# The value projections of two linear-attention branches as two stages of seven block products

## The chip, the cores and the metric

The kernel runs on one core of a Trainium2 chip. A core has a matrix engine (TensorE, PE in the profile; its weight loads, PEld, run beside the matmuls), VectorE (DVE), ScalarE (ACT), GpSimd (POOL) and SyncE (SP); here SP issues the loads and POOL most stores. Operands lie in SBUF, 128 partitions wide; matmuls accumulate in PSUM banks of 128 x 512 float32. The metric is the device time of one execution in microseconds, lower is better.

## The reference

One layer of a decoder trunk, 1024 rows (SEQ) by 1024 channels (D), in float32. The input is normalised and modulated, and one projection feeds two branches that run on the same normalised rows:

```python
h = rms_norm(x, norm_w[l]) * (1.0 + scale[:, None, :]) + shift[:, None, :]
proj = h @ w_in[l]
hq, hf, hi, hz, gq, gk, gv, gz, ga, mg = jnp.split(proj, IN_OFFSETS, axis=-1)
y_h = hgrn2_branch(hq, hf, hi, hz, lb_all[l], hgrn_norm_w[l])
y_g = gla_branch(gq, gk, gv, gz, ga, gla_alpha_w[l], gla_alpha_b[l], gla_norm_w[l])
u_h = y_h @ w_branch[l, 0]
u_g = y_g @ w_branch[l, 1]
mg = jax.nn.sigmoid(mg.reshape(B, T, N_BRANCH, D_MODEL))
merged = mg[:, :, 0] * u_h + mg[:, :, 1] * u_g
x = x + gate[:, None, :] * (merged @ w_out[l])
```

Both branches are causal linear attentions with a decay per key channel (8 heads of 128 channels in HGRN, 4 heads of 128 key and 256 value channels in GLA), `S_t = diag(a_t) S_{t-1} + k_t v_t^T`, `o_t = S_t^T q_t`. The change touches `v` alone: `gv` (GLA) and `hi` (HGRN), each the product of the 1024 x 1024 matrix h and a 1024 x 1024 part of `w_in`. In GLA the decay alpha comes from a rank-16 projection (`ga`) through a log-sigmoid.

## The kernel before

**Arithmetic.** Every float32 operand of a large product is split into a high and a low part in a shorter matmul format (`split`, L195: L200 casts on ACT, L201 subtracts on DVE), and a product is three matmuls: high x high, high x low, low x high. h, transposed, is kept whole in this form (`h_hi[k]`, `h_lo[k]`, eight tiles of 128 channels x 1024 rows each) and also, as float32, in DRAM (`h_d`).

**Memory.** SBUF is handed out as 46 slots of 4 KB per partition (`Slots`); a slot that comes free goes to a later tile, and a tile whose store is still under way is freed with `sent=True`, so that its slot is taken up again later than others. `Halves` (`Q`) gives out half slots. PSUM: two tiles of two banks (`dtile`, 128 x 1024, names pd), one more such tile for attention scores (`sc_ps`), and two of one bank (`mtile`, names pm).

**Stages.** First come normalisation, modulation and transposes. Then `first_group` (L488; its matmuls are L372) computes six feature groups of 128 channels side by side, the four heads of q and the first two of k of GLA, in six banks: `acc0` (both pd tiles) and `sc_ps`; `qk_out` (L351) copies each finished half to the tiles `qk_t`. Behind it runs a stream of jobs, `Stream.go`. A job has a `load` (raw weights by DMA), a `prep` (the hi/lo split) and a `run` (its matmuls, which yields after each unit); `ahead` does the loads and preps of coming jobs, as far as slots are free. After each unit `weave` advances two other tracks: `side` (decay chain `alpha_side`, then the attention of one head after another; a yielded number is the count of units to wait, run at PACE 1.1) and `back` (preparation of the last stages: factors, weight sums, gates).

The jobs, in order: `First` (the q/k group); for each GLA head its k projection (heads 2 and 3), two gate projections z, and its values; for each HGRN head q, f, z, with the values of four heads at once ahead of heads 0 and 4. A projection `Feat` (L581) is 8 x 2 x 3 = 48 matmuls of 128 x 512. A value job computes rows x channels, so that h is the stationary operand:
- `Vblk` (GLA, one head, 256 channels): 8 row blocks x 8 k-blocks x 3 matmuls of 256 columns (L640, L641, L642); four row blocks share a pd tile, which ACT copies to SBUF (L645). Its end starts the head's attention.
- `Vblk2` (HGRN, four heads, 512 channels): 8 x 8 x 3 matmuls of 512 columns (L683 to L685), two row blocks to a pd tile, copied by L688.

The first value matmul starts at 137.2 us and the last of the GLA branch at 365.6; those of the HGRN branch lie between 390.0 and 665.7.

Last come the gates, the branch projections and the output projection (L1387, L1564). These three 1024 x 1024 x 1024 products are computed as seven half-size products each instead of eight (`PRODUCTS`): four of the seven take sums of weight blocks (`w_sums`, made on DVE and stored to DRAM by the back track), four take differences of activation blocks (`f_x` for h, by `factors`), and results are combined from the accumulators and snapshots of them.

**Order.** The opening up to `first_group` follows an order written out by hand. Behind it the program order of jobs, `ahead` and `weave` is handed to a scheduler, which settles each engine's order. Each engine works through its own instructions in order; semaphores hold an instruction until what it needs is there.

## Time and profile before

| | |
|---|---|
| median of 3 runs | 1208.71 us (1207.79 to 1209.38) |
| the profiled execution | 1209.15 us, its span 1207.4 us |
| mean granted TensorE clock | 0.996 |

| stretch, us | length | PE busy | DVE busy | ACT busy | clock | GB/s |
|---|---|---|---|---|---|---|
| 0 to 109.5: opening, q/k group | 109.5 | 100.3 | 57.3 | 64.8 | 0.97 | 218 |
| 109.5 to 389.8: GLA stream | 280.3 | 278.5 | 167.8 | 121.4 | 1.00 | 119 |
| 389.8 to 802.4: HGRN stream | 412.6 | 412.0 | 273.4 | 157.3 | 1.00 | 121 |
| 802.4 to 1207.4: last stages | 405.0 | 395.3 | 288.4 | 204.9 | 1.00 | 188 |

An execution is profiled once; its span runs from the first to the last instruction that the profile shows, and the time of the execution contains a little more. Busy time counts an engine's instructions, overlaps once. In the timeline a row reads: start, duration, engine, line, operation, output <- inputs, shape, how many such rows in a run (x), and in brackets the idle time ahead of it and what ended that. Matmuls are pipelined: the duration of one is longer than the distance to the next.

### The profile page before, as it was taken

To read this page: it belongs to the slowest core of one execution; us is meant where nothing else is said; L and a number is where in the kernel's file an instruction comes from. 1 tells how busy PE (TensorE), PEld (TensorE's weight loads), DVE (VectorE), ACT (ScalarE), POOL (GpSimd) and SP (SyncE) were. 2 spreads that over 40 slices of the span, in tenths; PEclk is the share of its full clock that TensorE was granted. 3 is DMA by queue.
4 is the path that set the end of the run, shared out by engine and by line. 5 is a ranking of instruction groups with operands and counts; after the bars stand their busy time and mean duration, and the time that the engine had idled before them with its cause. 6 is when DMAs were issued, how large, how long until landed. Compare 5 with 4: busy or idle time off the path is not lost.

```text
span 1207.4 us, 20861 instructions
## 1 busy us (share of the span) xinstructions
PE 1186.1 (98%) x8617; PEld 990.0 (82%) x8617; DVE 786.9 (65%) x1210; ACT 548.3 (45%) x798; POOL 94.6 (8%) x204
## 2 busy tenths in 40 slices
PE   7999999999999999999999999999999999999997
PEld 6777889889798888888888888877878888878886
DVE  4737444774857556777965455795654865988994
ACT  5646732434434244234333324455743544444554
POOL 4100000101101012011100000000120000000000
PEclk8999999999999999999999999999999999999999
DMA  9814000844544167355441212154797846435423
GB/s 324 276 70 140 19 19 19 280 153 147 172 141 147 62 211 241 117 167 165 134 175 43 65 52 71 36 175 157 251 340 263 269 153 213 132 106 175 167 100 134
DMA packets 130960, 183.51 MB, mean 152 GB/s; under 512 B 7467, under 2 KB 97633, under 8 KB 130866
## 3 DMA queue, kind: packets, MB, share of 16 engines
q1 hardware_dynamic: 117250, 136.87, 36.3%
q0 software_dynamic: 13568, 45.31, 9.7%
q8 instruction: 67, 1.10, 0.4%
q14 instruction: 27, 0.22, 0.1%
q10 hardware_dynamic: 48, 0.01, 0.0%
HBM read 132.87 MB, written 49.28 MB: 151 GB/s over the span
## 4 chain that ended last, share of the span: by engine, by line
issue 58%; PE 30%; POOL 5%; DVE 2%; DMA 2%; ACT 1%; SPq 0%; POOLq 0%; DVEq 0%; ACTq 0%
PE pd L1387 9%; PE sc_ps L1387 5%; PE pm L1387 5%; PE pd L1564 3%; POOL ws L1244 2%; PE sc_ps L1564 2%; PE pm L1564 1%; PE pd L581 1%; DMA b<-in_w_in_dram 1%; POOL yh L956 1%; PE pd L372 1%; DMA b<-in_x_dram 1%; POOL yg L956 0%; DMA yg<-b 0%; POOL fx L1210 0%
## 5 line engine op out<-in xcount | busy, mean ns | idle before, releaser
L581 PE MATMUL pd<-b,b 128*128 128x512 f32 x1632 | 387.4, 394 | 0.0
L581 PEld LDWEIGHTS pd<-b,b 128*128 128x128 f32 x1632 | 302.4, 188 | 64.9 <-issue 1.4
L1387 PE MATMUL pd<-b,b 128*128 128x512 f32 x720 | 173.6, 392 | 2.7 <-DVE b L993 1.0
L1387 PEld LDWEIGHTS pd<-b,b 128*128 128x128 f32 x720 | 133.8, 188 | 33.8 <-ACT b L1458 2.1
L201 DVE TENSOR_TENSOR b<-b,b 128x1024 fp32r<-128x1024 f32 (+1 forms) x86 | 96.0, 1122 | 71.4 <-ACT b L200 57.7
L200 ACT CAST b<-b 128x1024 fp32r<-128x1024 f32 (+1 forms) x86 | 82.5, 970 | 91.5 <-PE pd L581 14.0
L1330 DVE TENSOR_TENSOR b<-b,b 128x1024 fp32r<-128x1024 f32 x56 | 68.4, 1222 | 58.4 <-ACT b L1329 37.9
L1329 ACT CAST b<-b 128x1024 fp32r<-128x1024 f32 x56 | 58.6, 1051 | 65.2 <-PE pm L1387 19.5
L1387 PE MATMUL sc_ps<-b,b 128*128 128x512 f32 x324 | 79.3, 391 | 0.3 <-ACT scT L833 0.3
L640 PE MATMUL pd<-b,b 128*128 128x256 f32 x256 | 74.2, 290 | 0.0
L1308 DVE TENSOR_TENSOR b<-b,b 128x1024 fp32r<-128x1024 f32 x48 | 57.7, 1220 | 23.3 <-ACT b L1307 15.5
L642 PE MATMUL pd<-b,b 128*128 128x256 f32 x256 | 72.5, 283 | 0.0
L641 PE MATMUL pd<-b,b 128*128 128x256 f32 x256 | 72.4, 283 | 0.0
L1387 PE MATMUL pm<-b,b 128*128 128x512 f32 x300 | 72.1, 389 | 0.0
L1387 PEld LDWEIGHTS sc_ps<-b,b 128*128 128x128 f32 x324 | 60.3, 188 | 13.8 <-ACT scT L833 0.7
L1307 ACT CAST b<-b 128x1024 fp32r<-128x1024 f32 x48 | 49.9, 1050 | 36.3 <-PE pd L1387 16.0
L1387 PEld LDWEIGHTS pm<-b,b 128*128 128x128 f32 x300 | 56.3, 188 | 11.7
L372 PE MATMUL pd<-b,b 128*128 128x512 f32 x192 | 52.4, 404 | 1.8 <-ACT b L200 1.1
L1244 POOL DMA_DIRECT2D ws<-b x64 | 34.5, 540 | 225.6 <-DVE b L1238 118.5
L774 ACT COPY xb<-b 128x512 f32<-128x512 f32 x48 | 29.3, 619 | 50.3 <-PE sc_ps L754 27.4
L683 PE MATMUL pd<-b,b 128*128 128x512 f32 x128 | 51.2, 400 | 0.0
L684 PE MATMUL pd<-b,b 128*128 128x512 f32 x128 | 49.9, 390 | 0.0
(298 smaller groups left out, 1943.5 us busy)
## 6 DMA issues: line engine op xcount, KB each, us to landing
b<-in_w_in_dram SPq DMA_DIRECT2D x66, 512.0 KB, 4.0
ws<-b POOLq DMA_DIRECT2D x64, 256.0 KB, 3.2
b<-ws SPq DMA_DIRECT2D x32, 512.0 KB, 4.2
b<-in_x_dram SPq DMA_DIRECT2D x16, 512.0 KB, 5.4
b<-in_ada_w_dram SPq DMA_DIRECT2D x32, 256.0 KB, 6.4
b<-in_w_branch_dram SPq DMA_DIRECT2D x16, 512.0 KB, 4.4
b<-h SPq DMA_DIRECT2D x14, 512.0 KB, 4.1
wo<-b POOLq DMA_DIRECT2D x14, 512.0 KB, 5.7
```

The costliest lines, as they stand in the source:

```text
L200: nc.scalar.copy(hi, src)
L201: nc.vector.tensor_sub(lo, src, hi.bitcast(F32))
L372: nc.tensor.matmul(accs[f], wg(a, d, f), b[d][:, half * 512:half * 512 + 512], start=(d == 0 and n == 0), stop=(d == KT - 1 and n == 2))
L581: nc.tensor.matmul(ps[0:w, th * 512:(th + 1) * 512], a[:, k, 0:w], b[:, th * 512:(th + 1) * 512], start=(k == 0 and n == 0), stop=(k == KT ...
L640: nc.tensor.matmul(o, lh, hi[:, k % 4, :], start=(k == 0), stop=False)
L641: nc.tensor.matmul(o, lh, lo[:, k % 4, :], start=False, stop=False)
L642: nc.tensor.matmul(o, ll, hi[:, k % 4, :], start=False, stop=(k == KT - 1))
L1244: nc.gpsimd.dma_start(w_sums[b][i // 2][q][:, i % 2 * 512:i % 2 * 512 + 512], parts[p].rearrange("p k f -> p (k f)"))
L1329: nc.scalar.copy(hi, t)
L1330: nc.vector.tensor_sub(lo, t, hi.bitcast(F32))
L1387: nc.tensor.matmul(o, a[:, sl], c, start=(p in (1, 5) and kt == 0 and n == 0), stop=(kt == 3 and n == 2), skip_group_check=True)
L1564: nc.tensor.matmul(o, a, b, start=(p in (1, 5) and kt == 0 and n == 0), stop=(kt == 3 and n == 2), skip_group_check=True)
```

## The change

The two value projections become two stages of seven block products each, and the jobs `Vblk` and `Vblk2` go.

- **The products.** `Vstage` holds four accumulators, one for each of four row blocks, as the four banks of two pd tiles (row blocks 0 and 1 in the first tile, 2 and 3 in the second). A `Vjob` is half of one product: for each row block i two k-blocks with three matmuls of 512 columns, so 24 matmuls, and a stage has 14 such jobs. In a product's second job `after` deals with each bank as soon as its six matmuls are issued: ACT takes a snapshot or a result (`take`: L1712, or L1714 with a scale), or DVE combines it with a snapshot; the next product goes on in the same banks. That makes 28 reads of banks in each stage.
- **Results** go to DRAM (`v_d`) as 128 x 512 pieces. Attention loads the values of its head with `early`, 6 - `lead` units before it needs them.
- **First stage (GLA), directly behind the q/k group.** It loads the four quarters of its weights raw, and `prep` forms the weight sums in place on DVE. The six q/k tiles are stored to DRAM when complete (`qk_d`, by POOL) and their slots given free; the attention of each head loads its q and k from there (`load_qk`). `hT`, the float32 parts of h's second half, stay in SBUF as sources of the factors, which `make_factor` forms from the group's last steps on and stores to `f_x`; `factors` on the back track goes.
- **Second stage (HGRN), between the GLA gate projections and the HGRN projections.** Its weight sums are formed earlier by the back track (`v_sums`), stored and loaded again; factors come from `f_x`.
- **Side track.** The GLA decay chain `alpha_side` is made for two heads at a time: heads 0 and 1 directly behind the q/k group, heads 2 and 3 put in front of the back track in the first stage's tenth job. Attention of GLA head 0 starts in the thirteenth job, of the others behind the z job of the head before, of HGRN heads behind their f job. Units are counted at 1.1 for GLA and 1.15 for HGRN (before 1.1 for both). Nothing is woven into the q/k group any more.

```diff
-PACE = 1.1
+PACE, PACE_H = 1.1, 1.15
...
         nc.scalar.copy(ga4[:, half * 512:half * 512 + 512], pg)
-        S.free(*[hT[half, i] for i in range(4)])
+        if half == 0:
+            S.free(*[hT[half, i] for i in range(4)])
...
                 if d == KT - 1:
                     qk_out(f, 1, accs[f])
+                    nc.gpsimd.dma_start(qk_d[f], qk_t[f])
+                    S.free(qk_t[f], sent=True)
...
-    class Vblk:
...
-        raws, parts = 2, 4
...
-                        nc.tensor.matmul(o, lh, hi[:, k % 4, :], start=(k == 0), stop=False)
-                        nc.tensor.matmul(o, lh, lo[:, k % 4, :], start=False, stop=False)
-                        nc.tensor.matmul(o, ll, hi[:, k % 4, :], start=False, stop=(k == KT - 1))
...
-    class Vblk2:
...
-        yield 10 - lead
+        yield 4
+        early()
+        yield 6 - lead
...
                 for u, _ in enumerate(job.run()):
-                    if u >= 3 and u % 2:
-                        self.ahead(i, loads, preps)
+                    if job.calls(u):
+                        self.ahead(i, loads + job.more, preps + job.more)
...
-    def factors(acts, f):
...
+    def load_wq(*at_):
+        wq[at_] = [S.get([2, 512]) for _ in range(2)]
+        for kk in range(2):
+            nc.sync.dma_start(wq[at_][kk], w_block(0, *at_, kk))
...
+    def make_factor(p, kk):
+        dst, x, y = {5: ("11", "12", "11"), 7: ("12", "12", "22"), 6: ("22", "22", "11"), 4: ("21", "21", "22")}[p]
+        nc.vector.tensor_sub(xq[dst][kk], xq[x][kk], xq[y][kk])
+        nc.gpsimd.dma_start(f_x[p][kk], xq[dst][kk].rearrange("p a t -> p (a t)"))
...
+    class Vstage:
...
+        def after(self, p, i):
+            bank, snap = self.bank[i], self.snap
+            if p == 1:
+                snap[1, i] = self.take(i, -1.0)
+            elif p == 2:
+                self.put(i, 0, 0, self.take(i))
+            elif p == 5:
+                snap[5, i] = self.take(i)
+            elif p == 3:
+                snap[3, i] = self.take(i)
+                nc.scalar.copy(bank, snap[1, i])
+                Q.free(snap.pop((1, i)))
+            elif p == 6:
+                t = snap.pop((3, i))
+                nc.vector.scalar_tensor_tensor(t, bank, -1.0, t, ALU.mult, ALU.subtract)
+                self.put(i, 0, 1, t)
+            elif p == 7:
+                t = snap.pop((5, i))
+                nc.vector.tensor_add(t, bank, t)
+                self.put(i, 1, 1, t)
+            elif p == 4:
+                self.put(i, 1, 0, self.take(i))
...
+        def prep(self):
...
+            if p == 5:
+                add(wq[0, 0][kk], wq[0, 0][kk], wq[0, 1][kk])
+                add(wq[0, 1][kk], wq[0, 1][kk], wq[1, 1][kk])
+            elif p == 3:
+                add(wq[0, 1][kk], wq[0, 0][kk], wq[1, 1][kk])
+                nc.vector.scalar_tensor_tensor(wq[1, 0][kk], wq[0, 1][kk], -1.0, wq[1, 0][kk], ALU.mult, ALU.subtract)
+            raw = wq[W_AT[p]][kk]
+            self.w = split(raw)
...
+            for i in range(4):
+                for a in range(2):
+                    x_hi, x_lo = self.x_part(a, i)
+                    w_hi, w_lo = (z[:, a, :] for z in self.w)
+                    for n, (x_, w_) in enumerate(((x_hi, w_hi), (x_hi, w_lo), (x_lo, w_hi))):
+                        nc.tensor.matmul(st.bank[i], x_, w_, start=(p in (1, 5) and kk == 0 and a == 0 and n == 0),
+                                         stop=(kk == 1 and a == 1 and n == 2), skip_group_check=True)
+                if kk:
+                    st.after(p, i)
+                yield
...
+    first_loads = {(2, 0): [lambda: load_wq(1, 0)],
+                   (2, 1): [lambda: load_wq(0, 1), lambda: load_wq(1, 1)],
+                   (6, 1): [lambda: load_xq(1)]}
...
+    vjobs[0][12].begins = first_head
+    vjobs[0][9].begins = lambda: stream.back.appendleft([alpha_side((2, 3)), 1, 1])
...
+    J.extend(vjobs[0])
...
+    J.extend(vjobs[1])
+    J.extend(hgrn)
+
+    def front():
+        for i, _ in enumerate(first_group()):
+            if i == 15:
+                make_ga(1)
+                load_wq(0, 0)
+            elif i == 16:
+                load_xq(0)
...
+            elif i == 19:
+                stream.ahead(0, 0, 0)
+            elif i > 19:
+                make_factor(5 if i < 22 else 7, i % 2)
+        start_side(alpha_side((0, 1)))
+        stream.back.append([v_sums(), 60, 1])
+        stream.back.append([prepare(), 4, 1])
+        stream.back.append([gate_side(), 4, 1])
```

The line numbers of new code are those of the changed kernel: L1714 is the read of product 1's banks in `take`, L1824 the matmul of a `Vjob`, L1659 the load of raw weights, L502 the store of a q/k tile, L1669 the store of a factor. The engines' orders show the three places that matter for the first stage. In the rows b_ and a number is an SBUF slot's tile, and "waits" names the engines or DMA queues whose semaphores the instruction waits for.

**PE, at the end of the q/k group.** Before, the group's last matmuls and the first job of the stream (a z projection, L581):

```order
L372 MATMUL pd_174<-b_146,b_162 128x512 [waits DVE_49]
L372 MATMUL pd_174<-b_154,b_162 128x512
L372 MATMUL pd_174<-b_146,b_166 128x512
L372 MATMUL sc_ps<-b_154,b_168 128x512
L372 MATMUL sc_ps<-b_146,b_170 128x512
L581 MATMUL pd_1068<-b_139,b_857 128x512 [waits DVE_49]
L581 MATMUL pd_1068<-b_139,b_857 128x512
L581 MATMUL pd_1068<-b_147,b_857 128x512 x2
L581 MATMUL pd_1068<-b_139,b_858 128x512 x2
```

In the change, the second job of product 1 in the first stage: pd_1080 and pd_1081 are the two tiles of two banks, and b_1096 and b_1097 the high and low weights. The six matmuls of row block 0, into pd_1080, stand ahead of these rows:

```order
L1824 MATMUL pd_1081<-b_1096,b_142 128x512
L1824 MATMUL pd_1081<-b_1097,b_142 128x512
L1824 MATMUL pd_1081<-b_1096,b_150 128x512
L1824 MATMUL pd_1080<-b_1096,b_141 128x512 [waits Activation_49]
L1824 MATMUL pd_1080<-b_1097,b_141 128x512
L1824 MATMUL pd_1080<-b_1096,b_149 128x512
L1824 MATMUL pd_1080<-b_1096,b_142 128x512
L1824 MATMUL pd_1080<-b_1097,b_142 128x512
L1824 MATMUL pd_1080<-b_1096,b_150 128x512
L1824 MATMUL pd_1081<-b_1096,b_141 128x512 [waits Activation_49]
```

The first three rows end row block 2 (pd_1081, first bank). Then row block 1, in pd_1080's second bank, waits for ACT, and row block 3, in pd_1081's second bank, waits for ACT again: each tile's second bank stands behind the read of its first. Before, the 48 matmuls of a job went on in one tile without such a wait.

**ACT, at the start of the stream.** Before, the decay chain of heads 0 and 1 (L969 bias, L977 Exp, L980 Ln, L984 Exp) between casts of weights (L200):

```order
L969 ACTIVATE b_1000<-pm_1002,vec 128x512
L969 ACTIVATE b_1000<-pm_1005,vec 128x512
L200 CAST b_1105<-b_986 128x1024
L200 CAST b_1173<-b_1066 128x1024
L977 ACTIVATE b_1000<-b_1000 128x1024
L980 ACT_TABLE_LOAD
L980 ACTIVATE b_1000<-b_1000,ones 128x1024
L984 ACT_TABLE_LOAD
L984 ACTIVATE b_1001<-b_1001 128x1024
L200 CAST b_1279<-b_1140 128x1024
L715 COPY xb<-b_680 128x32x32
```

In the change the chain's lines are L890 (bias), L901 (Exp) and L904 (Ln); L1714 are the reads of the first product's banks; b_1076 and b_1077 are raw weights of product 2:

```order
L200 CAST b_1100<-b_1076 128x1024
L890 ACTIVATE b_1135<-pm_1136,vec 128x512
L200 CAST b_1156<-b_1077 128x1024
L890 ACTIVATE b_1135<-pm_1139,vec 128x512
L901 ACTIVATE b_1116<-b_1116 128x1024
L904 ACT_TABLE_LOAD
L904 ACTIVATE b_1116<-b_1116,ones 128x1024
L1714 ACTIVATE b_1154<-pd_1080 128x512
L1714 ACTIVATE b_1176<-pd_1081 128x512
L901 ACT_TABLE_LOAD
L901 ACTIVATE b_1135<-b_1135 128x1024
L1714 ACTIVATE b_1154<-pd_1080 128x512
```

The casts of product 2's weights and half of the chain now stand ahead of the first read of a bank, and more of the chain between the reads. Before, no read of a bank that PE needs stood there.

**SP, the loads at the same place.** Before, the loads of the stream's first jobs (L563 projections, L617 values):

```order
L563 DMA b_986<-in_w_in_dram 128x8x128 [waits DMAHW4_49,DVE_49,PE_49]
L617 DMA b_1064<-in_w_in_dram 128x4x256 [waits DVE_49,PE_49]
L617 DMA b_1066<-in_w_in_dram 128x4x256 [waits DMASW5_49,DVE_49,PE_49]
L563 DMA b_1140<-in_w_in_dram 128x8x128 [waits DMAHW7_49,PE_49]
L563 DMA b_1224<-in_w_in_dram 128x8x128 [waits DMAHW4_49,DMAHW0_49,DVE_49]
L617 DMA b_1438<-in_w_in_dram 128x4x256 [waits DMAHW6_49,DMAHW1_49,DVE_49]
```

In the change, the raw weights of product 1 (b_996, b_997), two parts of h for the factors (b_1006, b_1007), and the raw weights of products 2, 5 and the later ones:

```order
L1659 DMA b_996<-in_w_in_dram 128x2x512 [waits DMASW7_49,DMAHW3_49,DVE_49,PE_49]
L1659 DMA b_997<-in_w_in_dram 128x2x512 [waits DMASW4_49,DMAHW4_49,DVE_49,PE_49]
L1664 DMA b_1006<-h_112 128x1024 [waits DMAHW5_49,DMASW5_49,PE_49]
L1664 DMA b_1007<-h_113 128x1024 [waits DMAHW6_49,DMASW6_49,PE_49]
L1659 DMA b_1076<-in_w_in_dram 128x2x512 [waits DMAHW7_49,DMASW6_49,DVE_49]
L1659 DMA b_1077<-in_w_in_dram 128x2x512 [waits DMAHW0_49,DMASW7_49,DVE_49]
L1659 DMA b_1088<-in_w_in_dram 128x2x512 [waits DMAHW1_49,DMASW0_49]
L1659 DMA b_1089<-in_w_in_dram 128x2x512 [waits DMAHW2_49,DMASW1_49,DVE_49]
L1659 DMA b_1092<-in_w_in_dram 128x2x512 [waits DMAHW3_49,DMASW2_49,DVE_49]
L1659 DMA b_1093<-in_w_in_dram 128x2x512 [waits DMAHW4_49,DMASW3_49,DVE_49]
```

The six loads from b_1076 on wait for stores of POOL's queue (DMASW): they take the slots of the six q/k tiles, whose stores to DRAM (L502) must have read them first. Before, of the loads shown one waited for such a store.

378 lines of the change are left out of this document (210 added, 168 removed).

## The prediction

> **What bounds the kernel now.** I read the page's first part, then the waits of TensorE (PE), then the PE rows of the two value computations that the change replaces, and last the PE timeline inside them.
>
> ```profile
> span 1207.4 us, 20861 instructions
> PE 1186.1 (98%) x8617; PEld 990.0 (82%) x8617; DVE 786.9 (65%) x1210; ACT 548.3 (45%) x798; POOL 94.6 (8%) x204
> ...
> PE pm L399 <- DVE b L214: 4.3, 2, 2.9
> ...
> PE pd L1387 <- DVE b L993: 1.0, 1, 1.0
> ...
> PE pd L1387 <- ACT b L1458: 1.0, 2, 0.7
> ```
>
> PE is busy for 98% of the span, and its waits (line, releaser, us in total, times, longest) are a few microseconds in all, the largest in the first 10 us. VectorE (DVE) and ScalarE (ACT) have slack. So the time is the length of the matmul stream plus PE's waits: a microsecond of stream removed is a microsecond gained, unless a new wait takes its place.
>
> ```profile
> L640 PE MATMUL pd<-b,b 128*128 128x256 f32 x256 | 74.2, 290 | 0.0
> L642 PE MATMUL pd<-b,b 128*128 128x256 f32 x256 | 72.5, 283 | 0.0
> L641 PE MATMUL pd<-b,b 128*128 128x256 f32 x256 | 72.4, 283 | 0.0
> ...
> L683 PE MATMUL pd<-b,b 128*128 128x512 f32 x128 | 51.2, 400 | 0.0
> L684 PE MATMUL pd<-b,b 128*128 128x512 f32 x128 | 49.9, 390 | 0.0
> L685 PE MATMUL pd<-b,b 128*128 128x512 f32 x128 | 49.9, 390 | 0.0
> ...
> 137.21 0.28 PE L640 MATMUL pd<-b,b 128*128 128x256 f32 x1
> 137.32 0.28 PE L641 MATMUL pd<-b,b 128*128 128x256 f32 x1
> 137.45 0.28 PE L642 MATMUL pd<-b,b 128*128 128x256 f32 x1
> 137.57 0.29 PE L640 MATMUL pd<-b,b 128*128 128x256 f32 x1
> ...
> 390.04 0.39 PE L683 MATMUL pd<-b,b 128*128 128x512 f32 x1
> 390.27 0.39 PE L684 MATMUL pd<-b,b 128*128 128x512 f32 x1
> 390.50 0.39 PE L685 MATMUL pd<-b,b 128*128 128x512 f32 x1
> 390.72 0.39 PE L683 MATMUL pd<-b,b 128*128 128x512 f32 x1
> ```
>
> The groups show 768 matmuls of 256 columns and 384 of 512, and no wait ahead of them. Their mean durations overlap; what they cost is the distance of their starts. Of 256 columns: (137.57 - 137.21)/3 = 0.120 us. Of 512: (390.72 - 390.04)/3 = 0.227 us. A 512-column matmul costs less than two of 256.
>
> **The change, part by part.**
>
> *The products.* Removed: 768 x 0.120 + 384 x 0.227 = 92.2 + 87.2 = 179.4 us. Added: two stages of seven products, each of 2 halves x 4 row blocks x 2 k-blocks x 3 = 48 matmuls of 512 columns, so 672 x 0.227 = 152.5 us. That is **-26.9 us** of stream: 12.8 from seven instead of eight products and 14.1 from the wide form of the first branch. Attention, projections and the last stages keep their matmuls.
>
> *Handoffs of banks, the added wait.* The four accumulators of a stage lie in two tiles of two banks. In the order of PE (in the part on the change) the six matmuls of one bank are followed by six of the other tile, and then the first tile's second bank waits for ACT: for the read of its first bank. So a read must end within 6 x 0.227 = 1.36 us. The trace has two such places.
>
> ```profile
> 884.81 1.05 ACT L1329 CAST b<-b 128x1024 fp32r<-128x1024 f32 x1 [2.29 <-DMA b<-in_w_in_dram]
> 885.77 0.62 ACT L1458 ACTIVATE b<-b 128x512 f32<-128x512 f32 x1
> 886.30 0.58 ACT L1458 ACTIVATE b<-pd 128x512 f32<-128x512 f32 x1
> ...
> 885.17 1.07 PE L1387 MATMUL pm<-b,b 128*128 128x512 f32 x4
> 886.93 3.01 PE L1387 MATMUL pd<-b,b 128*128 128x512 f32 x12 [0.69 <-ACT b L1458]
> ...
> 106.79 1.28 DVE L351 TENSOR_SCALAR b<-pd 128x512 f32<-128x512 f32 x2
> ...
> 107.53 1.64 PE L372 MATMUL pd<-b,b 128*128 128x512 f32 x6 [0.44 <-DVE b L351]
> ...
> 109.46 1.55 PE L581 MATMUL pd<-b,b 128*128 128x512 f32 x6
> ```
>
> A read of a bank takes 0.58; the matmul restarts 0.05 after its end (886.88 to 886.93), and the last matmul before ends 0.39 - 0.227 = 0.16 after its successor could start. An undisturbed handoff needs 0.16 + 0.58 + 0.05, about 0.8 of the 1.36 us: it is hidden, with some 0.55 us to spare. A read that stands behind one cast of 1.05 us, begun just ahead of it, is 0.5 us late; on average half of that. At 886.93 a cast and another operation stood in front, and PE lost 0.69 us.
>
> *The start of the first stage.* There ACT has the decay chain of the first two heads (the alpha rows) in front of the first reads, and the raw weights of products 2 and 5 arrive late: they go into slots of the six q/k tiles, which are first written to DRAM.
>
> ```profile
> 98.71 1.25 ACT L969 ACTIVATE b<-pm,vec 128x512 f32<-128x512 f32 x2
> 99.84 1.05 ACT L200 CAST b<-b 128x1024 fp32r<-128x1024 f32 x1
> ...
> 102.09 1.06 ACT L977 ACTIVATE b<-b 128x1024 f32<-128x1024 f32 x1
> 103.17 1.28 ACT L980 ACT_TABLE_LOAD   x1
> 104.46 1.15 ACT L980 ACTIVATE b<-b,ones 128x1024 f32<-128x1024 f32 x1
> ...
> b<-in_w_in_dram SPq DMA_DIRECT2D x66, 512.0 KB, 4.0
> ...
> h<-b POOLq DMA_DIRECT2D x8, 512.0 KB, 3.4
> fx<-b POOLq DMA_DIRECT2D x8, 512.0 KB, 6.5
> ```
>
> Count from the first matmul behind the first group (109.46 before). The first q tile is complete 2.0 us ahead of it (106.79 + 0.69 to 107.48). Its 512 KB store has no row; h and fx, of the same size, land in 3.4 and 6.5, and I take 4.5, nearer to h since the fx stores are mostly through by then: +2.5. The load behind it takes 4.0: +6.5. The second q tile is complete at about -0.2 (the second pair of L351 before), its weights are there at +8.3. ACT, in its order: cast to 7.6, bias 0.68 to 8.3, cast to 9.4, bias to 10.1, Exp 1.06 to 11.1, table 1.28 to 12.4, Ln 1.15 to 13.6, first read to 14.2. PE gets there after 42 matmuls of 512 (0.227) and the five small ones of the chain (some 1.2 us): 10.7. **It waits 3.5.** Then second-bank matmuls run from 14.2 to 16.9, while ACT does a read, a table load, an Exp and a read (0.6 + 1.28 + 1.06 + 0.6) to 17.7: **0.8**. Table, Ln and read to 20.8, against PE's 20.4: **0.4**. The next 22 matmuls end at 25.8; two casts, a table load, two Exp, a cast and the read of product 2 end at 27.9: **2.1**. Sum **6.8 us**. The bounds: 0 if the reads come through, and about 13 if loads and stores, 6 MB within some 15 us, land 6 us later.
>
> Here the row and the Trainium skill differ. ScalarE: Activation LUTs, What ACT_TABLE_LOAD costs, adds a drain of some 1.4 us to the load's 1.28. The rows have none: 102.09 + 1.06 ends at 103.15, the load runs from 103.17, and the Ln starts at 104.46, 0.01 behind it. With that drain at each of the four table loads the start would lose about 5.5 us more, and the sum would be 1201; I go by the row.
>
> *The other reads.* Both stages have 56; eight are in the start. In the order of ACT and DVE I count 26 of the other 48 with another operation between the end of the bank and its read. At 0.24 each (half of 0.5): **+6 us**, from 0 (all hidden) to 26 x 0.69 = 18.
>
> *Work beside the stream.* Casts and subtractions of hi/lo parts go from 16 to 44 pairs (1.05 on ACT, 1.22 on DVE).
>
> ```profile
> L201 DVE TENSOR_TENSOR b<-b,b 128x1024 fp32r<-128x1024 f32 x70 | 85.1, 1221 | 41.3 <-ACT b L200 27.5 <-PE pd L642 6.6 <-DMA yh<-b 3.4
> ...
> 109.50:389.80 280.30, 278.48 (x2462) 246.35 (x2461) 167.84 (x277) 121.37 (x159) 21.48 (x40) 1.00 0.37 119
> 389.80:802.40 412.60, 411.95 (x3680) 344.13 (x3679) 273.36 (x477) 157.28 (x247) 33.44 (x62) 1.00 0.38 121
> ```
>
> The two windows (length; busy PE, weight loads, DVE, ACT, POOL; clock; DMA) cover the stream behind the first group: 692.9 us with 441 of DVE and 279 of ACT. DVE gets 28 x 1.22 for splits, 16 x 1.22 for weight sums and 16 reads of 0.69, 65 us together, and six of its eight factor subtractions move ahead of this stretch; 499 of 679 us is 73%. ACT gets 28 x 1.05 and 48 copies of 0.59 for 16 of 1.01, 41 us: 320 of 679. Both stay covered by the stream; if the cover failed, DVE would have to fall a job behind, priced below. The six early subtractions, 6 x 1.22, stand on DVE ahead of the q/k reads, in a stretch where DVE idled before (PE's last group, 95 to 106): nothing. The value stores and loads (32 stores of 256 KB, 16 MB both ways with the loads) add to 183.5 MB at a mean of 152 GB/s, and each head asks for its values some 10 us ahead: nothing.
>
> Sum, from the profiled execution's own 1209.15 us (1.75 around its span, 0.04% above the median of the runs, 1208.71): 1209.15 - 26.9 + 6.8 + 6 = 1195, and 1 us for waits of the heads, which follow each other more closely than before: **1196 us**.
>
> **The rivals.**
>
> *All waits hidden.* If weights land early and the reads slip in between, only the products count: 1209.15 - 26.9 = 1182, up to 1186. For it: the old stages wait at their banks for about 2 us in all. Against it: there a bank has 12 matmuls, 2.7 us, not 1.36.
>
> *The reads eat the gain (slower).* The place is the handoff of the banks. Each of the 56 reads would have to cost over 26.9/56 = 0.48 us for the sign to turn; at the 0.69 of 886.93 for 48 of them and 13 at the start it is -26.9 + 33 + 13 = +19, 1228 us. For it: ACT and DVE take their operations in order, and the second stage shares them with attention. Against it: at most half the reads have something ahead.
>
> *A clock that falls.*
>
> ```profile
> 10.00:20.00 10.00, 7.14 (x40) 6.32 (x40) 3.81 (x10) 4.42 (x10) 4.37 (x21) 0.71 1.06 367
> ```
>
> After PE's early waits the granted clock was 0.71 in this window, and 1.00 in both windows above. A wait of 3.5 us in the start could repeat it: 10 us at 0.71 cost about 3 us, 1199. TensorE: Matmul & The Clock Gate of the Trainium skill, What's actually happening, has the clock halve after an idle window of about 3.4 us; by that rule the start is just at the edge, and the trace shows no full idle window inside the stream to test it.
>
> *DVE becomes the bound.* Around the last GLA heads and the second stage it is densest. If it falls one job (10.9 us of 48 matmuls) behind there, that is 1207, no change.
>
> That the products aren't shortened can be left out: the order of PE has the 672 matmuls.
>
> **How the numbers follow.** Forecast with waits of 8 to 18 us, 1190 to 1201: 0.45. All hidden, up to 1188: 0.20. Clock: 0.08, near 1199. More waits at the reads, still a gain, 1201 to 1206: 0.08. DVE, or waits that equal the gain: 0.09. Slower: 0.10. The range leaves out the best of the hidden case and most of the slow one: 1184 to 1211. What can be told from no change begins at about 0.2%, 2.4 us: faster 0.80, same 0.10, slower 0.10.
>
> **What will show it.** Right: 672 matmuls spaced 0.227; PE waits on ACT reads at the first stage's start, 4 to 10 us in all, the first over 2 us; small ones elsewhere; DVE near 850 us. Wrong: PE waiting there for DMA or DVE in the first place, tens of microseconds at the reads, a clock below 1.00 behind the start, or values of a head that arrive late.

## The result and the profile after

| | before | change |
|---|---|---|
| median | 1208.74 us | 1248.92 us (1247.76 to 1249.91, 4 runs) |
| ratio | | 1.0333, 95% interval 1.0315 to 1.0351 |
| span of the profiled execution | 1207.4 us | 1247.9 us |

The change is 40 us slower. The forecast was 1196 us: a stream shorter by 27 us, less 14 us of new waits. The profile's first part, and the change's stages as windows (length; busy PE, weight loads, DVE, ACT, POOL; clock; DMA share; GB/s), from the end of the q/k group on: first stage, GLA projections, second stage, HGRN projections, last stages.

```profile
span 1247.9 us, 20244 instructions
PE 1183.1 (95%) x8137; PEld 959.3 (77%) x8137; DVE 845.6 (68%) x1270; ACT 578.9 (46%) x853; POOL 119.7 (10%) x250
...
107.90:205.30 97.40, 87.97 (x412) 66.08 (x412) 66.39 (x81) 64.50 (x78) 9.57 (x19) 0.96 0.49 167
205.30:352.30 147.00, 144.19 (x1201) 119.51 (x1196) 98.43 (x161) 56.20 (x80) 16.30 (x31) 1.00 0.58 188
352.30:478.10 125.80, 111.78 (x859) 90.39 (x858) 72.24 (x116) 58.73 (x93) 12.89 (x24) 0.97 0.46 149
478.10:842.70 364.60, 344.52 (x3194) 284.65 (x3193) 261.57 (x465) 139.17 (x221) 35.88 (x66) 0.97 0.47 150
842.70:1247.90 405.20, 395.92 (x1977) 323.41 (x1975) 287.78 (x343) 205.61 (x286) 17.16 (x32) 1.00 0.56 190
```

Length less busy PE is PE's idle time: 9.4, 2.8, 14.0, 20.1 and 9.3 us. Of the stream's part of the span (the first four stretches) 46 us are idle; before it was 2.5. The clock is below 1.00 in three of them: busy time times what the clock lacks, summed over windows of 1 us, is 2.8, 0, 2.9, 10.2 and 0, in all 15.9 us. Before it was 0.0 there. So 44 us of idle and 16 of clock stand against the shorter stream. PE busy at full clock fell by 18.7 us over the whole span, where 26.9 had been forecast; 44 + 16 - 19 is the difference of the spans, 40.5, within 1 us.

PE's longest waits (line, releaser, us in total, times, longest):

```profile
PE sc_ps L642 <- DVE xb L638: 11.8, 3, 5.1
PE pd L1824 <- ACT b L1714: 6.9, 2, 5.4
PE pd L1824 <- ACT pd L1732: 6.4, 2, 5.1
PE pd L1824 <- ACT b L1712: 4.6, 4, 2.0
...
PE pm L928 <- DVE b L201: 3.7, 1, 3.7
```

The largest row is not at the banks (L1824, 20.8 us in all its rows together) but at the opening of three HGRN heads (L642, the first score matmuls, which need DVE's L638). One of these three in the timeline:

```profile
555.32 0.92 SPq L1127 DMA_DIRECT2D b<-in_w_branch_dram  x2
556.34 0.45 SPq L566 DMA_DIRECT2D b<-in_w_in_dram  x1
564.40 0.37 SPq L1127 DMA_DIRECT2D b<-in_w_branch_dram  x1
...
561.55 0.86 DVE L637 TENSOR_TENSOR xb<-xb,b 128x512 f32<-128x512 f32 x1
567.84 0.69 DVE L1134 TENSOR_TENSOR b<-b,b 128x512 f32<-128x512 f32 x1 [5.43 <-DMA b<-in_w_branch_dram]
568.45 0.63 DVE L638 TENSOR_TENSOR xb<-xb,b 128x256 f32<-128x256 f32 x1
...
569.23 2.36 PE L642 MATMUL sc_ps<-xb,b 128*32 128x80 f32 x64 [5.11 <-DVE xb L638]
```

L1134 is an addition of the branch weight sums (back track). It stands in DVE's order between two steps of the head's opening and waits 5.43 us for its load (L1127), which SP issued 8 us after the one ahead of it; L638 and PE wait with it. Why SP issued it late stands in its own waits between 556 and 565 us:

```profile
SPq L1127 <- DMA yh<-b: 7.5, 1, 7.5
```

The load takes a slot whose last tile, a result of attention (yh), was still on its way to DRAM. That store was issued at 556.9, beside three loads and another store, and landed at 564.3; the load itself then took 3.3 us.

The five waits of 1.9 us or more make 17.5 of the 20.1 us in the HGRN stretch. Three of them (3.72 us at 485.4, 4.53 at 518.2 and the one shown) stand behind an addition that waits for a sum's late load. Ahead of the other two (2.18 at 617.6, 1.98 at 681.5) stands the split of a projection weight, L201, for which DVE stood idle 2.91 and 4.19 us; in the second of them the cast before it had waited 8.86 us for its load.

The second stage has a wait of the same kind at its banks: a cast of a stored weight sum waits 4.18 us for its load, with the reads of the banks behind it on ACT.

```profile
420.82 0.32 SPq L1766 DMA_DIRECT2D b<-vs  x1
424.69 1.04 ACT L200 CAST b<-b 128x1024 fp32r<-128x1024 f32 x1 [4.18 <-DMA b<-vs]
425.64 1.07 ACT L1712 COPY b<-pd 128x512 f32<-128x512 f32 x2
426.60 1.12 ACT L1732 COPY pd<-b 128x512 f32<-128x512 f32 x2
427.25 1.22 PE L1824 MATMUL pd<-b,b 128*128 128x512 f32 x2 [5.05 <-ACT pd L1732]
```

At the start of the first stage the first wait came as forecast, but longer: two casts of late weights and the decay chain stand ahead of the first read.

```profile
103.12 1.37 DVE L351 TENSOR_SCALAR b<-pd 128x512 f32<-128x512 f32 x2 [0.65 <-PE pd L373]
...
115.20 1.05 ACT L200 CAST b<-b 128x1024 fp32r<-128x1024 f32 x1 [3.04 <-DMA b<-in_w_in_dram]
116.16 0.68 ACT L890 ACTIVATE b<-pm,vec 128x512 f32<-128x512 f32 x1
118.58 1.04 ACT L200 CAST b<-b 128x1024 fp32r<-128x1024 f32 x1 [1.75 <-DMA b<-in_w_in_dram]
...
122.47 1.15 ACT L904 ACTIVATE b<-b,ones 128x1024 f32<-128x1024 f32 x1
123.53 1.06 ACT L1714 ACTIVATE b<-pd 128x512 f32<-128x512 f32 x2
...
124.16 11.02 PE L1824 MATMUL pd<-b,b 128*128 128x512 f32 x36 [5.37 <-ACT b L1714]
```

### The profile page after: what moved, and what is told of

The parts are those of the page before. It is cut to its first block, busy times and chain, and to the rows that moved or that the text cites. A ratio compares the mean times of both kernels' runs of the same rounds, so it can differ in the third digit from the quotient of the medians.

```text
span 1247.9 us, 20244 instructions
## 1 busy us (share of the span) xinstructions
PE 1183.1 (95%) x8137; PEld 959.3 (77%) x8137; DVE 845.6 (68%) x1270; ACT 578.9 (46%) x853; POOL 119.7 (10%) x250
## 3 DMA queue, kind: packets, MB, share of 16 engines
q0 software_dynamic: 18144, 61.04, 12.8%
## 4 chain that ended last, share of the span: by engine, by line
issue 46%; PE 25%; POOL 5%; DVE 1%; DMA 1%; ACT 0%; POOLq 0%; DVEq 0%; SPq 0%
PE pd L1281 10%; PE pm L1281 5%; PE sc_ps L1281 5%; PE pd L1458 3%; POOL ws L1139 3%; PE sc_ps L1458 2%; PE pm L1458 1%; POOL yh L875 1%; POOL v L1719 1%; POOL yg L875 1%; DMA gate<-b 0%; DMA v<-b 0%; DMA b<-in_w_in_dram 0%; POOL gate L1353 0%; DVE b L1198 0%
## 5 line engine op out<-in xcount | busy, mean ns | idle before, releaser
L584 PE MATMUL pd<-b,b 128*128 128x512 f32 x1632 | 396.5, 399 | 0.0
L584 PEld LDWEIGHTS pd<-b,b 128*128 128x128 f32 x1632 | 306.7, 191 | 65.7 <-issue 0.7
L201 DVE TENSOR_TENSOR b<-b,b 128x1024 fp32r<-128x1024 f32 (+1 forms) x114 | 129.9, 1149 | 104.8 <-ACT b L200 77.8
L1824 PE MATMUL pd<-b,b 128*128 128x512 f32 x672 | 172.9, 410 | 20.8 <-ACT b L1714 6.9
L1281 PE MATMUL pd<-b,b 128*128 128x512 f32 x720 | 173.6, 392 | 2.0 <-ACT b L1255 1.2
L1824 PEld LDWEIGHTS pd<-b,b 128*128 128x128 f32 x672 | 127.0, 193 | 56.6 <-ACT b L1712 7.7
L200 ACT CAST b<-b 128x1024 fp32r<-128x1024 f32 (+1 forms) x114 | 111.2, 989 | 116.5 <-DMA b<-in_w_in_dram 40.7
L1281 PEld LDWEIGHTS pd<-b,b 128*128 128x128 f32 x720 | 133.7, 188 | 33.5 <-ACT b L1255 2.6
L1281 PEld LDWEIGHTS sc_ps<-b,b 128*128 128x128 f32 x324 | 60.3, 188 | 13.9 <-ACT b L1253 0.6
L915 ACT ACTIVATE b<-pd 128x1024 f32<-128x1024 f32 x24 | 24.6, 1027 | 66.0 <-PE pd L584 65.9
L373 PE MATMUL pd<-b,b 128*128 128x512 f32 x192 | 51.7, 402 | 0.5 <-ACT b L200 0.5
L807 PE MATMUL pm<-scT,b 128*128 128x128 f32 x256 | 47.5, 277 | 2.6 <-DVE b L794 2.6
L373 PEld LDWEIGHTS pd<-b,b 128*128 128x128 f32 x192 | 34.5, 188 | 12.4 <-issue 1.3
```

Of the source, the lines that this page charges most:

```text
L200: nc.scalar.copy(hi, src)
L201: nc.vector.tensor_sub(lo, src, hi.bitcast(F32))
L373: nc.tensor.matmul(accs[f], wg(a, d, f), b[d][:, half * 512:half * 512 + 512], start=(d == 0 and n == 0), stop=(d == KT - 1 and n == 2))
L584: nc.tensor.matmul(ps[0:w, th * 512:(th + 1) * 512], a[:, k, 0:w], b[:, th * 512:(th + 1) * 512], start=(k == 0 and n == 0), stop=(k == KT ...
L1281: nc.tensor.matmul(o, a[:, sl], c, start=(p in (1, 5) and kt == 0 and n == 0), stop=(kt == 3 and n == 2), skip_group_check=True)
L1824: nc.tensor.matmul(st.bank[i], x_, w_, start=(p in (1, 5) and kk == 0 and a == 0 and n == 0), stop=(kk == 1 and a == 1 and n == 2), skip_g ...
```

## The experiments

Theory A: additions of weight sums that wait for late loads, in DVE's order inside a head's opening, make the waits of the HGRN heads. Its rivals are B, the heads follow their projections too closely; C, loads hold each other up in SP's queue. Other runs ask for the waits of the two stages. Each cell of the table is PE's idle time plus the clock loss, in us, in the stage's own window of the profiled execution; each ratio is to runs of the kernel before beside it (1208.2 to 1209.6 us).

| run | us | ratio (95%) | first stage | second stage | HGRN |
|---|---|---|---|---|---|
| the change | 1248.92 | 1.0333 (1.0315 to 1.0351) | 9.4+2.8 | 14.0+2.9 | 20.1+10.2 |
| e1 sums ahead | 1234.32 | 1.0222 (1.0201 to 1.0243) | 9.9+2.6 | 10.4+4.4 | 11.8+2.5 |
| e2 pace | 1249.14 | 1.0333 (1.0296 to 1.0371) | 9.5+2.6 | 12.6+4.1 | 19.7+8.1 |
| e3 no sums | 1219.18 | 1.0087 (1.0069 to 1.0104) | 10.2+2.6 | 9.2+0.0 | 2.8+0.0 |
| e4 alpha later | 1255.68 | 1.0396 (1.0361 to 1.0432) | 15.7+5.0 | 14.8+2.7 | 19.9+7.3 |
| e5 e1, sums by POOL | 1243.42 | 1.0292 (1.0275 to 1.0309) | 9.6+3.8 | 13.0+4.4 | 19.7+2.0 |
| e6 weights early | 1254.03 | 1.0376 (1.0358 to 1.0393) | 12.1+5.4 | 14.8+5.4 | 19.0+8.9 |
| e7 reads in pairs | 1245.04 | 1.0300 (1.0277 to 1.0322) | 9.7+4.6 | 8.3+4.7 | 22.4+6.2 |
| e8 = e1+e6+e7 | 1229.68 | 1.0168 (1.0141 to 1.0195) | 12.8+3.2 | 10.2+3.0 | 7.9+4.4 |
| e9 chain placed | 1247.68 | 1.0324 (1.0302 to 1.0346) | 13.0+1.6 | 10.5+1.4 | 17.4+9.1 |
| e10 e1, values by POOL | 1234.89 | 1.0216 (1.0190 to 1.0242) | 10.5+2.9 | 10.7+5.8 | 12.0+3.8 |
| e10b e1, SP in program order | 1236.60 | 1.0243 (1.0216 to 1.0270) | 10.6+2.6 | 10.8+1.5 | 16.3+2.5 |
| e12 e1, sums faster | 1266.06 | 1.0475 (1.0447 to 1.0504) | 10.4+3.2 | 13.9+4.6 | 24.4+4.1 |
| e13 first stage alone | 1228.98 | 1.0175 (1.0151 to 1.0200) | 9.4+3.9 | | 13.1+4.5 |
| e14 second stage alone | 1256.39 | 1.0393 (1.0372 to 1.0414) | | 17.3+3.0 | 13.9+4.9 |
| e15 sums on POOL | 1267.47 | 1.0491 (1.0471 to 1.0512) | 10.7+2.5 | 12.0+2.1 | 32.5+12.0 |
| e16 = e1+e7+e15 | 1259.44 | 1.0419 (1.0398 to 1.0440) | 9.1+3.3 | 10.2+6.0 | 32.6+11.0 |
| e17 before, short lead | 1225.90 | 1.0148 (1.0130 to 1.0165) | | | 12.8+3.7 |
| e18 e1, weights ahead | 1235.22 | 1.0222 (1.0204 to 1.0240) | 9.7+3.0 | 12.6+3.1 | 11.1+4.4 |

### The weight sums and the heads

```diff
# e1: prepare() loads sum n+1 ahead of the additions of sum n
+            if n < 15:
+                xs[n + 1] = load_sums(*todo[n + 1])
             yield 6
+            x1, x2 = xs.pop(n)
# e2
-PACE, PACE_H = 1.1, 1.15
+PACE, PACE_H = 1.1, 1.1
# e3: no loads, no additions; a tile of zeros is stored instead
+                yield 7.5
+                for p, q in SUMS.items():
+                    nc.gpsimd.dma_start(w_sums[b][i // 2][q][:, i % 2 * 512:i % 2 * 512 + 512], z[:, 0:512])
```

> The loads of the branch weight sums are issued one sum ahead of their additions (some 10 units, 14 us, more lead); the work is the same. Theory A (weight-sum additions stand in DVE's order inside the opening of an HGRN head and wait there for late loads, and PE waits for DVE): of the 20.1 us of PE idle and 10.2 us of clock loss between 478 and 843 us at least half goes, about 1233 us or less. Rival B (heads follow their f projection too closely, whatever stands between): idle there stays at 16 us or more, 1244 to 1252 us.

> Only the pace of the HGRN heads goes back from 1.15 to 1.10. Rival B (heads too dense): PE idle in the HGRN stretch, 20.1 us, falls by half or more and the time to 1233 us or less. Theory A (late loads of weight sums): idle there stays between 14 and 26 us, the time between 1242 and 1254 us, apart from what a newly drawn order shifts.

> Leaves out the loads and additions of the weight sums for the gates and branch projections: zeros are stored in their place, with the same stores. Theory A: PE idle in the HGRN stretch falls from 20.1 to under 6 us and its clock loss from 10.2 to under 2, the time to about 1222 us. Rival B (heads too close) and rival C (SP held up by the loads of a head's values): 14 us of idle or more stay, 1238 us or more.

Without loads and additions of the sums the HGRN stretch has 2.8 us of idle and a full clock, as in the row:

```profile
472.00:809.20 337.20, 334.36 (x3194) 277.34 (x3193) 233.35 (x417) 138.99 (x220) 10.23 (x19) 1.00 0.29 84
```

So all but 3 of the 30 us hang on the sums, and rival B falls: the heads are as close there as in the change, and a slower pace (e2) changes nothing. But e3 takes away the additions, the loads, their traffic and their slots at once, so it doesn't tell by which of these the sums act. With more lead for the loads 14.6 us go (e1); the redrawn order of e1 has also moved three of the four additions out of the heads' openings. The reverse was tried on the kernel before, where the loads' lead was cut from 6 to 2 units:

```diff
# e17, on the kernel before: weight_sums
-        yield 6
+        yield 2
...
-        yield 3
+        yield 7
```

> The kernel before, with the loads of a weight sum 2 instead of 6 units ahead of its additions (and 7 instead of 3 units behind them, so that the sums keep their places). Theory A (the lead of the loads decides whether the sums hold up the heads, and the kernel before has enough): waits of PE in the heads appear, 10 us or more, 1220 us or more. If the lead doesn't matter by itself: 1207 to 1211 us.

It became 17.7 us slower, but not by the way of Theory A. The longest of PE's new waits:

```profile
473.96 1.04 ACT L200 CAST b<-b 128x1024 fp32r<-128x1024 f32 x1 [8.00 <-DMA b<-in_w_in_dram]
475.04 1.23 DVE L201 TENSOR_TENSOR b<-b,b 128x1024 fp32r<-128x1024 f32 x1 [3.65 <-ACT b L200]
476.18 0.68 DVE L782 TENSOR_TENSOR b<-b,tot 128x512 f32<-128x512 f32 x1
476.92 1.75 PE L847 MATMUL pm<-ident,b 128*128 128x128 f32 x7 [7.04 <-DVE b L782]
```

Ahead of the head's step L782 stands no addition but the split of a projection weight, whose load is late. SP issued that load at 465.5, right behind one of a sum (L1232) that had waited 5.0 us for its slot, and it took 8.3 us, where the median of such loads is 4.3 in this stretch. The second wait, 2.29 us at 511.1, stands behind such a split too. So the time at which the sums' loads are issued matters by itself, but in the two longest waits no addition stood in the way: another load came late. Whether SP's order, the slots or the traffic delayed it, the rows don't separate.

What DVE's additions of sums waited for their loads before (two rows) and in the change (four):

```profile
DVE b L1239 <- DMA b<-in_w_branch_dram: 8.1, 2, 4.8
DVE b L1239 <- DMA b<-in_w_in_dram: 0.5, 1, 0.5
```

```profile
DVE b L1133 <- DMA b<-in_w_in_dram: 9.5, 4, 3.5
DVE b L1134 <- DMA b<-in_w_in_dram: 7.1, 3, 5.8
DVE b L1134 <- DMA b<-in_w_branch_dram: 7.0, 2, 5.4
DVE b L1133 <- DMA b<-in_w_branch_dram: 2.8, 1, 2.8
```

With a third row of 0.4 us these are 9.0 us before and 26.4 in the change. Yet DVE's whole idle time ahead of these two additions is nearly the same, 28.6 and 30.4 us (before, other releasers ended most of it), and a wait of 4.8 us for such a load at 446.8 before cost PE nothing. What differs as well is the place: in the change an addition stands between L637 and L638, in the opening of a head, in four of eight HGRN heads, before in one, where its load had landed. That the sums make the waits is shown; how much of it is the loads' lateness and how much the redrawn order, is not.

### By which way late loads reach PE

```diff
# e5, on e1: load_sums
-            nc.sync.dma_start(x.rearrange("p k a f -> p k (a f)"),
+            nc.gpsimd.dma_start(x.rearrange("p k a f -> p k (a f)"),
# e10, on e1: a head's values (GLA alike)
-            nc.sync.dma_start(v[0], v_d[1][:, h * P:(h + 1) * P]
+            nc.gpsimd.dma_start(v[0], v_d[1][:, h * P:(h + 1) * P]
# e10b, on e1: loads of projections, sums and HGRN values each as
+            tc.keep_in_program_order(nc.sync.dma_start(...
# e12, on e1
-        stream.back.append([v_sums(), 60, 1])
-        stream.back.append([prepare(), 4, 1])
+        stream.back.append([v_sums(), 120, 2])
+        stream.back.append([prepare(), 4, 2])
# e15, on the change: weight_sums
-        add = nc.vector.tensor_add
+        add = nc.gpsimd.tensor_add
# e18, on e1
+    for job in hgrn:
+        job.more = 1
```

> As the run with the weight sums' loads one sum ahead (1234 us), but these loads are issued by POOL, so that they no longer stand in SP's queue. Theory C (SP holds the loads of projection weights and values behind a weight-sum load whose slot is not free yet): the 11.8 us of idle and 2.5 us of clock loss that were left in the HGRN stretch fall under 6 and 1 us, about 1226 us. Rival (only the lead of the loads counts): 1230 to 1238 us.

> As the run with the weight sums' loads one sum ahead (1234 us, HGRN stretch 11.8 us idle and 2.5 clock), but the loads of a head's values are issued by POOL. Theory C1 (a value load that waits on SP holds up the projection weights behind it): 11.8 and 2.5 fall to 6 and 1 or less, 1226 us. If it is the hoisted weight-sum loads that hold SP up: 1231 to 1238 us.

> As the run with the weight sums' loads one sum ahead (1234 us), but SP issues the loads of projections, weight sums and HGRN values in the order in which the program writes them; before, the scheduler had put some weight-sum loads ahead of loads that are needed sooner. Theory C2 (loads that were pulled forward wait on SP for their slots and hold up others): the HGRN stretch falls from 11.8 and 2.5 us to 6 and 1 or less, 1226 us. If the order on SP doesn't matter: 1231 to 1238 us. If program order is worse than the drawn one, more.

> As the run with the weight sums' loads one sum ahead (1234 us), and the back track goes twice as fast while it makes sums, from the same unit on: in DVE's order 14 of 16 weight sums now stand ahead of the first HGRN head, instead of 6. Theory A (weight sums among the openings of the HGRN heads make the waits there): the HGRN stretch falls from 11.8 us idle and 2.5 us clock loss to 5 and 1 or less, while the GLA stretch (3.5 us idle) may take up to 5 more; 1222 to 1229 us. Rival (the sums' total load on DVE and the DMA queues, wherever they stand): what HGRN gains the GLA stretch and the second stage lose, 1232 us or more.

> The change with one difference: the additions of the branch weight sums run on POOL (10% busy) instead of DVE, with the same loads and stores, so that an addition that waits for its load no longer stands ahead of a head's opening on DVE. Theory A (late loads act through DVE's order): the HGRN stretch falls from 20.1 us idle and 10.2 clock loss to 6 and 2 or less, 1226 us or less. Rival (late loads act through SP's queue, which also delays the projection weights): 10 us of idle or more stay, 1234 us or more.

> As the run with the weight sums' loads one sum ahead (1234 us), and in the HGRN projections weights are loaded three jobs ahead instead of two and split two jobs ahead instead of one. Theory D (loads that land late are the common cause: whichever stands behind a late load in ACT's or DVE's order, the split of a projection weight or a sum, holds up the head): more lead for the second class too takes the HGRN stretch from 11.8 us idle and 2.5 clock loss to 5 and 1 or less, 1223 to 1228 us. Rival (transfers are late because there are too many of them or because SP waits for slots, so that asking earlier doesn't help): 10 us of idle or more stay, 1232 us or more.

None came under the 1234 us of e1, so none of the forecasts of A, C and D for these runs held. In e12 the sums stand earlier in DVE's order, but their loads are not earlier: DVE stood for one, and PE waited 19 us for the head behind it. In e15, with the additions off DVE, the waits grew, and the longest came by another class of loads, the projection weights, whose split stands in the heads' order too (DVE was also slower beside POOL, see the last section, so e15 is no clean test of DVE's order):

```profile
535.67 1.12 SPq L566 DMA_DIRECT2D b<-in_w_in_dram  x2
541.62 1.04 ACT L200 CAST b<-b 128x1024 fp32r<-128x1024 f32 x1 [15.13 <-DMA b<-in_w_in_dram]
542.75 1.23 DVE L201 TENSOR_TENSOR b<-b,b 128x1024 fp32r<-128x1024 f32 x1 [12.13 <-ACT b L200]
...
544.99 0.70 PE L731 MATMUL sc_ps<-xb 128*16 128x16 f32 x62 [9.63 <-DVE blk L717]
```

So what the rows show is wider than A: whatever waits for a late load in ACT's or DVE's order ahead of a head's step holds up PE. An addition of a sum is one such instruction, not the only one. Why the loads are late is settled only in part: moving one class to POOL (e5, e10), keeping SP in program order (e10b) and asking earlier for the projection weights (e18) each left 11 to 20 us of idle. Slots that are not free yet when SP reaches a load are one cause in the rows: 7.5 us for a store of yh in the change, 12.8 us for a store of a sum ahead of the load at 535.67 in e15. Traffic is another in part: in the HGRN stretch the projection weights (512 KB each) landed a median 5.9 us after their issue, before 4.0, while the sums' loads (L1127; L1232 before) were no slower, 3.7 us and 4.2 before. How much either cause costs was not tried alone.

### The first stage and the banks

```diff
# e4
-        start_side(alpha_side((0, 1)))
+    vjobs[0][5].begins = lambda: start_side(alpha_side((0, 1)))
# e6: raw weights of product 2 at i == 16 of the q/k group, parts of h with job (2, 0)
-                load_xq(0)
+                load_wq(1, 0)
...
-    first_loads = {(2, 0): [lambda: load_wq(1, 0)],
+    first_loads = {(2, 0): [lambda: load_xq(0)],
# e7
-                if kk:
+                if kk and i % 2:
+                    st.after(p, i - 1)
                     st.after(p, i)
# e9, on e6: the chain starts with product 5, each step kept in program order between two products
+    vjobs[0][4].begins = lambda: start_side(alpha_side((0, 1), 8 * PACE))
```

> The decay chain of GLA heads 0 and 1 starts in the sixth job of the first stage instead of ahead of it; the work is the same. If the chain is what delays the first reads: the first wait of PE in the stage, 5.4 us, falls to 2 us or less and its 2.8 us of clock loss goes, 1240 us. If the late raw weights of product 2 alone do it (their casts stand ahead of the reads): the wait stays at 3 to 5 us, 1244 to 1249 us.

> The raw weights of product 2 are loaded before the end of the q/k group, in slots that are free then; the two parts of h for the factors take their place in the slots of the q/k tiles, and the first two factors are formed with product 5. If late raw weights, whose casts stand ahead of the reads on ACT, make the first wait: 5.4 us fall to 1.5 or less, the clock loss of 2.8 us goes, 1241 us. If the decay chain is as long by itself: 3 us or more of the wait stay, 1245 us or more.

> Both banks of an accumulator tile are read behind the matmuls of both, so that no second bank waits for the read of the first: half as many waits, each with 12 matmuls (2.7 us) of cover instead of 6 (1.36 us). If the handoff of the banks is what the second stage waits for: its idle falls from 14.0 to 8 us or less, that of the first stage from 9.4 to 6 or less, time 1240 us or less. Rival (late loads and attention in ACT's and DVE's order, whatever the cover): the second stage keeps 12 us or more, 1244 to 1250 us.

> Three edits together: weight-sum loads one sum ahead, product 2's weights early, reads in pairs. If they act on different waits and add up: 1248.9 less 14.6 (measured), 6 and 8 (expected), about 1220 us. If what one takes away another wait takes back: 1228 us or more.

> First stage alone: product 2's raw weights early (as in the run before), and the decay chain of heads 0 and 1 begins with product 5 and is held in ACT's order at the places between two products, where no bank waits to be read; the chain of heads 2 and 3 comes behind the stage. If both, late casts and the chain in front of the reads, make the waits of the first stage, each enough by itself: its 9.4 us of idle and 2.8 of clock loss fall to 4 and 0.5 or less, 1241 us. If the handoffs of banks themselves cost it: 8 us or more stay, 1247 us or more.

> Sums on POOL, their loads one sum ahead, and the banks read in pairs. If the three act on different waits: HGRN stretch 5 us idle or less, second stage 8 to 10, first stage 9 to 10 with 3 to 5 of clock loss: 1215 to 1222 us. If waits come back elsewhere: 1228 us or more. To come under the kernel before, 1209 us, the first stage would have to lose most of its waits, which none of these edits does.

Both e4 and e6 came out slower than the change. Each of the two causes at the start is enough by itself: with the chain later the late weights' casts still make a wait of 4.1 us, and the chain makes another of 5.1 where it now stands; with the weights early the chain makes one of 4.9. With both out of the way (e9) the first waits are 1.1 and 1.3 us, but 13.0 us of idle are spread over the stage. Its rest is the handoff of banks: reads there stand behind casts of weights whose loads or slots are late, or wait for a slot themselves (the longest two, 2.6 and 4.2 us, for a stored piece of values to leave its slot). In pairs the second stage's idle falls from 14.0 to 8.3, nearly as expected, but its clock loss rises from 2.9 to 4.7, the first stage gains nothing, and the time, 1245 us, is the rival's. The edits add up only in part: e8, at 1229.68 the fastest of those with both stages that do all of the work, is still 1.7% slower than the kernel before. e16 shows the loss of e15 again.

### One stage at a time

e13 keeps the change's first stage and computes the HGRN values by the eight-product jobs of before; e14 keeps the second stage, with the GLA values as before and factors and sums on the back track.

> Only the first half of the change: GLA values by seven products as in the change, HGRN values by eight products of two jobs inside the stream as before, no second set of weight sums. Matmul stream 15.9 us shorter than before (92.2 less 76.3). If the first stage costs what it costs in the change (9.4 idle, 2.8 clock) and the HGRN heads are undisturbed again: 1204 to 1209 us. If the HGRN heads wait as in the change (20 us idle, 10 clock) even without the second stage: 1225 us or more.

> Only the second half: GLA values by eight products inside the stream as before, HGRN values as the second stage ahead of the HGRN projections, with its factors and weight sums from the back track. Matmul stream 10.9 us shorter than before (87.2 less 76.3). If stage and HGRN heads wait as in the change (17 and 30 us): 1240 to 1250 us. If the waits of the HGRN heads came from the first stage, which delays the back track: 1212 to 1222 us.

Either stage alone is slower than the kernel before, by 20 and 48 us, and in both the heads wait (13.1 and 13.9 us of idle). So the heads' waits come with any of the two, not with one edit; that the order which the scheduler then draws anew does it is argued, not shown.

## Why the prediction was wrong

- **The stream: right.** The matmuls of the stages are spaced 0.227 us (median of all starts), and there are 672. Of the 26.9 us 18.7 show as fewer busy microseconds; PE stops 25 times in the stream instead of 6, and each stop leaves the pipeline's 0.16 us in the busy time, 3 us. The other 5 us are not accounted for.
- **The start of the first stage: right in mechanism, near in size.** A table load took 1.28 us without a drain, as the forecast chose to count it (121.18, the next ACT instruction at 122.47). The first wait was 5.4 us, not 3.5. The first q tile is complete at 104.5, which puts the zero of the forecast's count at 106.5; the two weights then came at +8.7 and +12.1 instead of +6.5 and +8.3. The three later waits (0.8, 0.4, 2.1) did not come; two of 1.7 and 1.2 us came at the stage's end. The whole stage has 9.4 us, and 6.8 and some 2.5 for the other 20 of its reads had been forecast; that the sums agree is luck in part, since the waits came at other places.
- **The other reads: mis-sized.** +6 us for 48 reads, 28 of them in the second stage, so some 3.5; it has 14.0 (8.3 in pairs), 12 of them at its banks. Half of the 0.5 us by which one cast delays a read was the price; a cast that waits for its own load costs its wait, 5.05 us at one bank.
- **Waits of the heads, 1 us: this step failed.** It is 20.1 us in the HGRN stretch alone, with 10.2 of clock. Its reason was "Both stay covered by the stream" from 73% of DVE and 320 of 679 us of ACT, and "nothing" for transfers from a mean rate. DVE was as busy as forecast (845.6 us against "near 850", 72% in the HGRN stretch); what counted was which instruction stood ahead of a head's step and when its load landed or its slot came free. The five longest waits of the stretch show it, and e3 shows that without the sums they go.
- **The transfers, "nothing": undercounted too.** 16 MB more were forecast. The profile's page has 220.2 MB, 36.7 more than before: besides the values, the q/k tiles and the second stage's sums go out and come back, and the factors are loaded twice. What these bytes alone cost was not tried.
- **The clock: a rival taken as a single case.** 3 us at one place, the start, were priced, and 2.8 came there. But the clock also fell behind each of the other five waits over 2 us and behind two places with shorter ones, in all 15.9 us.
- **The slower rival: the right sign, the wrong place.** It set the price at the banks, where PE's idle time ahead of L1824 is 20.8 us in all, less than the 26.9 us of the forecast stream; the heads and the clock made the sign.
- What the prediction named as a sign against itself came: a clock below 1.00 behind the start, and some 20 us of waits at the reads.

## What to carry to other kernels

An engine's free time does not cover an instruction that stands in order behind one that waits for a load: for each place where the bound engine waits for another, read what stands ahead there, when its load was issued and landed, and which slot that load waited for, before writing "nothing". Where a scheduler draws the orders, a change in one stage redraws the others; the term for the untouched stages is then the most uncertain one, and here it was the largest loss. A wait of the matmul engine is to be priced with the clock that it may cost: in the streams of these runs every wait of 3.4 us or more was followed by a clock of 0.50, of those between 2 and 3.4 us some were and some were not.

## What the runs showed of the hardware

**The clock.** Around the wait of 5.11 us above, in windows of 2 us:

```profile
564.00:566.00 2.00, 0.12 (x1) 0.00 (x0) 0.00 (x0) 0.00 (x0) 0.00 (x0) 1.00 0.27 79
566.00:568.00 2.00, 0.00 (x0) 0.00 (x0) 0.16 (x1) 0.00 (x0) 0.00 (x0) 0.65 0.57 194
568.00:570.00 2.00, 0.77 (x24) 0.80 (x28) 2.00 (x4) 0.00 (x0) 0.54 (x1) 0.50 0.04 14
570.00:572.00 2.00, 2.00 (x49) 1.78 (x42) 1.86 (x4) 0.92 (x2) 0.00 (x0) 0.50 0.30 117
572.00:574.00 2.00, 2.00 (x7) 1.53 (x7) 2.00 (x5) 0.00 (x0) 0.00 (x0) 0.64 0.00 0
```

PE is idle from 564.1 to 569.2. The records of the granted clock behind these means hold only 1.00 and 0.50 in this run, and each fall in the stream lasts 3.4 or 6.8 us. With these two values the mean of 0.65 puts the fall at 566.6, 2.5 us into the wait, and 0.64 the end at 573.4, 4.2 us behind it: this wait cost some 2 us more. The Trainium skill, TensorE: Matmul & The Clock Gate, What's actually happening, has two states and windows of about 3.4 us, of which an idle one halves the clock; 6.8 us at 0.50 are two such windows, which agrees. But a wait of 2.2 us at 615 also brought 0.50, without an idle window of that length, and one of 1.95 us at 401 did not; in e3 waits of 2.30, 2.45 and 2.72 us did not either.

**DVE beside POOL.** In e15 DVE's operations took two to three times as long where POOL added at the same time: L637 1.92 us instead of 0.86 above, L644 1.66 instead of 0.60.

```profile
624.58 1.36 POOL L1134 TENSOR_TENSOR b<-b,b 128x512 f32<-128x512 f32 x1 [1.52 <-DMA b<-in_w_branch_dram]
624.75 1.66 DVE L644 TENSOR_TENSOR b<-b,b 128x256 f32<-128x256 f32 x1
625.91 1.63 POOL L1136 TENSOR_TENSOR b<-b,b 128x512 f32<-128x512 f32 x1
626.33 1.92 DVE L637 TENSOR_TENSOR xb<-xb,b 128x512 f32<-128x512 f32 x1
```

The Trainium skill, Trainium Architecture — The Big Picture, What this means for kernel authors, names a port pair that the two share, with an exclusive lock; these rows agree: both of DVE's operations end behind the addition that POOL had begun before them, by 0.5 and 0.7 us.
